# A matmul's opening: A's k-tiles 8 to 15 in two lots, B by two k-tiles, the bias loaded and added later

## The chip, the cores and the metric

One core of one Trainium2 chip. The metric is the device time of one execution in microseconds (us). The span in a profile counts from the first to the last instruction and is shorter: by 1.7 us in the runs of the kernel before. The times before spread little on the first chip (1781.77 to 1782.03 us).

## The reference

```python
a = randn(4096, 4096)      # float32
b = randn(4096, 4096)
bias = randn(4096)
out = tanh(a @ b + bias)
```

## The kernel before

fp16 matmuls of 128 x 128 by 128 x 512. B is worked in four chunks of 1024 columns, A in 32 row blocks of 128 rows, K in 32 k-tiles of 128. Row blocks are called 0 to 31. For the first chunk neither B nor A is there at the start, so the first eight row blocks are an **opening**: group 0 (row blocks 0 to 3) and group 1 (4 to 7) take the k-tiles in stretches as they land, and partial sums are set aside in SBUF (`spill`). All loads but those of B's first two k-tiles stand in one software queue issued by GpSimd (`want`, `want_a`), with at most eight in flight (counted from issue to landing in the trace of before, up to 95 us); VectorE transposes A (`turn`), adds partial sums (`add_aside`), adds the bias (`add_bias`) and the result (`end`). VectorE's timelines below show its instructions in the order of the program.

```python
    want_a("g0b", G, 0, G * Q, BL, BL)             # group 0, k-tiles 4-7
    want_a("g0c", G, 0, G * Q, KS, KM - KS)        # group 0, k-tiles 8-15, one lot
    for u in range(KS, KM, 2):
        want(lambda u=u: load_b_all(u, 2))         # B by two k-tiles, four loads each
    want_a("g1c", 2, 4 * P, 2 * Q, KS, KM - KS)    # group 1, k-tiles 8-15
    want_a("g1d", 2, 6 * P, 2 * Q, KS, KM - KS)
    bias_bc = biasp.tile([P, NCW], fp32, name="bias_bc")
    want(lambda: load_bias(bias_bc, 0, nc.gpsimd))
    for t in (KM, KM + 8):                         # 16 and 24
        want_a(("g1", t), G, 4 * P, G * Q, t, 8)
        for u in range(t, t + 8, TB):
            want(lambda u=u: load_b_all(u, TB))    # B by four k-tiles
    for m in g0:
        want_a(("g0", m), 1, m * P, Q, KM, KT - KM)
    # ... cut ...
    one_by_one(ps, g1, KS, KM, KS)
    for t in (KM, KM + 8):
        for i in range(G):
            turn(ats[G + i], ("g1", t), i * Q, t, 8)
        for m in g1 if t == KM else g0:
            for j in range(J):
                add_bias(m, j)
        across(ps, g1, t, min(t + 8, KT - TB), KS)
    turn(ats[0], ("g0", 0), 0, KM, KT - KM)        # row block 0, k-tiles 16-31
    down(ps, g1, KT - TB, KT, end)                 # group 1's results
    # ... cut ...
    for m in g0:
        for j in range(J):
            ps = psum.tile([P, NB], fp32, name="ps")
            for t in range(KM, KT):
                mm(ps, ats[m], b_cur, t, j, t == KM, t == KT - 1)
            if m < G - 1 and j == 0:
                turn(ats[m + 1], ("g0", m + 1), 0, KM, KT - KM)
            elif m == G - 1:
                new_at(j)
            end(ps, m, j)
```

## Time and profile before

| | before |
|---|---|
| time, median of 3 | 1781.81 us |
| TensorE busy, of a span of 1780.2 us | 1774.4 us |
| steady start-to-start of two matmuls in the opening | 0.216 us |
| waits of TensorE in the opening after 25 us, beyond that step | 0.08 + 0.21 + 0.24 us |
| landing of row block 0's last k-tiles | 84.88 us |
| first matmul of row block 1 on k-tiles 16 to 31 | 98.22 us |

To read it: TensorE is the bound, and the whole question is how long it stands still in the first 119 us. Its timeline of the kernel before, 84 to 110 us (start, length, engine, line and operation), merges what follows without a break:

```profile
83.76 7.72 PE L138 MATMUL ps<-b,at 128*128 128x512 f16 x35
91.31 18.94 PE L138 MATMUL ps<-b,atx 128*128 128x512 f16 x87
```

The second line is row blocks 0 to 2 of group 0 on k-tiles 16 to 31, without a pause. A line with a pause before it would carry a bracket with its length and who ended it.

### The profile page before, as it was taken

How to read it: one execution, taken by the hardware profiler on the slowest of the kernel's cores; microseconds unless marked ns; L12 is line 12 of the kernel's file. 1: busy time of each engine (PE TensorE's matmuls, PEld its weight loads, DVE VectorE, ACT ScalarE, POOL GpSimd, SP SyncE). 2: the span in 40 equal slices, each digit the busy share in tenths (PEclk: the TensorE clock that was granted, in tenths of full speed). 3: DMA queues.
4: the chain of work that ended last, by engine and by line, in shares of the span. 5: the costliest groups of instructions: out<-in, count | busy, mean ns of one | idle time of the engine just before them, and what ended most of it. 6: DMA issues, size and time to landing. Idle time of an engine off the chain costs nothing.

```text
span 1780.2 us, 20854 instructions
## 1 busy us (share of the span) xinstructions
PE 1774.4 (100%) x8254; PEld 806.9 (45%) x8254; DVE 763.8 (43%) x680; ACT 173.2 (10%) x279; POOL 872.1 (49%) x1618
## 2 busy tenths in 40 slices
PE   9999999999999999999999999999999999999999
PEld 4444444444444444444444444444444444444444
DVE  3764353444344443444344443444344443444342
ACT  2011000000000000000000000000000000000001
POOL 7465566544466554444456554444544454444510
PEclk9999999999999999999999999999999999999999
DMA  9999999976999877767699987766776667766641
GB/s 186 203 189 178 168 166 169 140 124 109 165 165 173 148 115 115 119 114 121 113 177 165 170 137 115 119 115 109 129 117 120 107 114 115 120 114 109 116 77 42
DMA packets 281393, 238.94 MB, mean 134 GB/s; under 512 B 159056, under 2 KB 231760, under 8 KB 281296
## 3 DMA queue, kind: packets, MB, share of 16 engines
q0 software_dynamic: 243280, 167.88, 70.1%
q1 hardware_dynamic: 37728, 69.62, 11.0%
q8 instruction: 64, 1.05, 0.2%
q14 instruction: 33, 0.27, 0.0%
q10 hardware_dynamic: 288, 0.13, 0.0%
HBM read 337.64 MB, written 67.11 MB: 227 GB/s over the span
## 4 chain that ended last, share of the span: by engine, by line
PE 99%; DMA 0%; issue 0%; ACT 0%; POOL 0%; DVE 0%; DVEq 0%; POOLq 0%
PE ps L412 93%; PE ps L138 6%; DMA nat<-in_a_dram 0%; ACT o_sb L152 0%; PE tp L257 0%; POOL nat L246 0%; DVE o_sb L149 0%; DVEq L149 0%; POOLq L435 0%
## 5 line engine op out<-in xcount | busy, mean ns | idle before, releaser
L412 PE MATMUL ps<-b,at 128*128 128x512 f16 x7712 | 1657.8, 378 | 0.0
L90 POOL DMA_DIRECT2D an<-in_a_dram x1492 | 805.5, 547 | 796.6 <-DVE at L100 583.4
L412 PEld LDWEIGHTS <-at 128*128 128x128 f16 x7712 | 754.6, 98 | 903.3
L100 DVE STREAM_TRANSPOSE at<-an 128x512 f16<-128x512 f16 (+1 forms) x380 | 565.6, 1539 | 85.8 <-DMA an<-in_a_dram 85.8
L149 DVE TENSOR_TENSOR o_sb<-ps,bias_bc 128x512 f32<-128x512 f32 (+1 forms) x243 | 165.4, 683 | 897.7 <-PE ps L412 695.7
L152 ACT ACTIVATE o_sb<-o_sb 128x512 f32<-128x512 f32 (+1 forms) x243 | 151.8, 626 | 1499.1 <-DVE o_sb L149 1499.1
L73 POOL DMA_DIRECT2D b<-in_b_dram x104 | 56.2, 544 | 15.5 <-DMA an<-in_a_dram 8.4
L138 PE MATMUL ps<-b,atx 128*128 128x512 f16 x256 | 56.2, 379 | 0.0
L138 PE MATMUL ps<-b,at 128*128 128x512 f16 x256 | 55.7, 379 | 0.1
L138 PEld LDWEIGHTS <-at 128*128 128x128 f16 x256 | 25.0, 98 | 30.5 <-DVE spill L181 0.5
L138 PEld LDWEIGHTS <-atx 128*128 128x128 f16 x256 | 24.6, 98 | 30.1 <-DVE atx L100 0.9
L100 DVE STREAM_TRANSPOSE atx<-an 128x512 f16<-128x512 f16 (+2 forms) x12 | 16.3, 1399 | 13.0 <-DMA an<-in_a_dram 13.0
L69 POOL DMA_DIRECT2D b<-in_b_dram x12 | 7.8, 654 | 22.4 <-PE ps L412 22.3
L152 ACT ACTIVATE spill<-spill 128x512 f32<-128x512 f32 x16 | 9.9, 632 | 85.6 <-DVE spill L149 85.5
L149 DVE TENSOR_TENSOR spill<-ps,spill 128x512 f32<-128x512 f32 x16 | 10.4, 678 | 9.9 <-PE ps L138 9.9
L181 DVE TENSOR_TENSOR spill<-spill,bias_bc 128x512 f32<-128x512 f32 x16 | 9.7, 680 | 0.0
L173 ACT COPY spill<-ps 128x512 f32<-128x512 f32 x16 | 8.0, 623 | 12.9 <-PE ps L138 12.9
L228 PE MATMUL ps<-zeros 128*128 128x512 f16 (+1 forms) x14 | 4.7, 498 | 1.3 <-DVE zeros L221 1.3
L176 DVE TENSOR_TENSOR spill<-ps,spill 128x512 f32<-128x512 f32 x8 | 4.8, 670 | 0.0
L228 PEld LDWEIGHTS <-zeros 128*128 128x128 f16 x14 | 1.6, 130 | 3.7 <-issue 2.4
L239 DVE CAST b<-spill 128x1024 f16<-128x1024 f32 x1 | 0.8, 849 | 4.5 <-DMA spill<-in_b_dram 4.5
L246 POOL DMA_DIRECT2D nat<-in_a_dram x4 | 2.3, 587 | 0.8 <-POOLq L435 0.8
(14 smaller groups left out, 8.9 us busy)
## 6 DMA issues: line engine op xcount, KB each, us to landing
an<-in_a_dram POOLq DMA_DIRECT2D x480, 192.0 KB, 5.1
out_dram<-o_sb SPq DMA_DIRECT2D x239, 256.0 KB, 2.7
an<-in_a_dram POOLq DMA_DIRECT2D x960, 32.0 KB, 2.7
b<-in_b_dram POOLq DMA_DIRECT2D x94, 256.0 KB, 8.2
b<-in_b_dram POOLq DMA_DIRECT2D x6, 1024.0 KB, 13.5
an<-in_a_dram POOLq DMA_DIRECT2D x32, 128.0 KB, 5.6
out_dram<-spill SPq DMA_DIRECT2D x16, 256.0 KB, 5.9
an<-in_a_dram POOLq DMA_DIRECT2D x12, 256.0 KB, 8.2
```

Of the source, the lines that this page charges most:

```text
L69: queue.dma_start(out=dst, in_=src[:, ds(t0 % BL, nt), :])
L73: nc.gpsimd.dma_start(out=bt[t0 // TB][ds(q * QP, QP), ds(t0 % TB, nt), :], in_=src.rearrange("(t p) n -> p t n", p=QP),)
L90: nc.gpsimd.dma_start(out=an[ds(q * QP, QP), :, ds((t - t0) * QP, n * QP)], in_=src.rearrange("(mb p) k -> p mb k", p=QP),)
L100: nc.vector.transpose(at[:, ds(t, n), :].rearrange("P t (mb p) -> P mb t p", p=QP), an[:, ds(mb0, Q), ds((t - t0) * QP, n * QP)].rearrange ...
L138: nc.tensor.matmul(ps, at[:, t, :], bt[t // TB][:, t % TB, ts(j, NB)], start=start, stop=stop)
L149: nc.vector.tensor_tensor(out=o_sb[:, piece], in0=ps[:, piece], in1=addend[:, piece], op=mybir.AluOpType.add)
L152: nc.scalar.activation(o_sb[:, piece], o_sb[:, piece], mybir.ActivationFunctionType.Tanh)
L173: nc.scalar.copy(aside(m, j), ps)
L176: nc.vector.tensor_tensor(out=aside(m, j), in0=ps, in1=aside(m, j), op=mybir.AluOpType.add)
L181: nc.vector.tensor_tensor(out=aside(m, j), in0=aside(m, j), in1=bias_bc[:, ts(j, NB)], op=mybir.AluOpType.add)
L228: nc.tensor.matmul(ps[:, ds(0, w)], zeros[:, :P], zeros[:, :w], start=i == 0, stop=i == n - 1)
L412: nc.tensor.matmul(ps, at[:, t, :], b_cur[t // TB][:, t % TB, ds(c0, w)], start=t == 0, stop=t == KT - 1,)
```

## The change

The intent is to have each k-tile there before TensorE asks: group 0's k-tiles 8 to 15 in two lots with their share of B in between, B's k-tiles 16 to 19 and 24 to 27 in lots of two, and the bias out of the way of both, behind B's k-tile 27. Since the bias then lands late, its additions move too. The diff:

```diff
-    want_a("g0c", G, 0, G * Q, KS, KM - KS)
-    for u in range(KS, KM, 2):
-        want(lambda u=u: load_b_all(u, 2))
+    for t in (KS, KS + 4):
+        want_a(("g0", t), G, 0, G * Q, t, 4)
+        for u in (t, t + 2):
+            want(lambda u=u: load_b_all(u, 2))
...
-    want(lambda: load_bias(bias_bc, 0, nc.gpsimd))
     for t in (KM, KM + 8):
         want_a(("g1", t), G, 4 * P, G * Q, t, 8)
-        for u in range(t, t + 8, TB):
-            want(lambda u=u: load_b_all(u, TB))
+        for u in (t, t + 2):
+            want(lambda u=u: load_b_all(u, 2))
+        if t > KM:
+            want(lambda: load_bias(bias_bc, 0, nc.gpsimd))
+        want(lambda t=t: load_b_all(t + TB, TB))
...
-    for m in g0:
-        turn(ats[m], "g0c", m * Q, KS, KM - KS)
+    for t in (KS, KS + 4):
+        for m in g0:
+            turn(ats[m], ("g0", t), m * Q, t, 4)
...
-        for m in g1 if t == KM else g0:
-            for j in range(J):
-                add_bias(m, j)
         across(ps, g1, t, min(t + 8, KT - TB), KS)
+    for m in g1:
+        for j in range(J):
+            add_bias(m, j)
     turn(ats[0], ("g0", 0), 0, KM, KT - KM)
     down(ps, g1, KT - TB, KT, end)
+    for m in g0:
+        for j in range(J):
+            add_bias(m, j)
```

## The prediction

85.5 + 2.24 + 4.81 + 4.86 + 2.30 = 99.7, and with it the 1783.2 us, rests on the trace of before and on estimates from it. In that trace one bias addition lasts 0.685 us and the next starts after 0.60. The 0.72 us of part (1) is the mean step between landings of four loads of A with runs of 128 elements, 25.61 to 27.85 us. The DMA share is 1.24 in the mean from 25 to 90 us (1.10 to 1.30 by stretches). That what stands behind a load put later comes forward by its length, in part (3), was the estimate: about 2 us for the bias.

> **What bounds the kernel now.** I read the head of the page with the engine totals first:
>
> ```profile
> span 1780.2 us, 20854 instructions
> PE 1774.4 (100%) x8254; PEld 806.9 (45%) x8254; DVE 763.8 (43%) x680; ACT 173.2 (10%) x279; POOL 872.1 (49%) x1618
> ```
>
> Then the chain that ended last, in order of time (start, length, what ran):
>
> ```profile
> 9.79 25.99 PE ps L138 x120
> 35.78 0.05 issue
> 35.82 41.60 PE ps L138 x192
> 77.42 0.08 issue
> 77.50 41.60 PE ps L138 x192
> 119.10 1654.20 PE ps L412 x7680
> ```
>
> TensorE is busy for all but 5.8 us. From 9.79 us to the end the chain is matmuls, broken twice by less than 0.1 us. The breaks are a little wider in the start times of single matmuls, which otherwise stand 0.216 apart: 35.40 to 35.82 (0.43) and 77.05 to 77.50 (0.46). So the waits that an opening order can take away are 0.21 + 0.24 = 0.45 us. The kernel is bound by TensorE; an order of loads can win 0.45 us or lose what it newly exposes.
>
> What stands behind the two breaks is read from the landing records of the software queue's loads beside the program's waits. B's k-tiles 8 and 9 finish landing at 35.73 and the matmul starts at 35.82. B's k-tiles 24 to 27, one lot of four, land at 77.26 and the matmul starts at 77.50. The loads of the opening land back to back from about 25 to 90 us, so in that stretch the DMA engines are full and the order decides who waits. A (fp32 in HBM, 0.5 MB a load) takes 1.33 us a load, B in lots of two k-tiles 0.64, in lots of four 1.25.
>
> Next the VectorE timeline where the eight-row opening ends, 84 to 101 us (start, length, what, and idle time before it with who ended it), then GpSimd's in the same stretch:
>
> ```profile
> 85.07 2.31 DVE L100 STREAM_TRANSPOSE atx<-an 128x2048 f16<-128x2048 f16 x1 [3.85 <-DMA an<-in_a_dram]
> 87.31 4.90 DVE L149 TENSOR_TENSOR spill<-ps,spill 128x512 f32<-128x512 f32 x8
> 92.12 2.30 DVE L100 STREAM_TRANSPOSE atx<-an 128x2048 f16<-128x2048 f16 x1
> 94.97 0.69 DVE L149 TENSOR_TENSOR spill<-ps,spill 128x512 f32<-128x512 f32 x1 [0.55 <-PE ps L138]
> ```
>
> ```profile
> 94.72 4.30 POOL L90 DMA_DIRECT2D an<-in_a_dram  x8 [4.89 <-DVE atx L100]
> ```
>
> The reader is to see that VectorE has no pause from 85.07 to 94.42, and that it starts there only when a load lands. The second transpose makes row block 1's k-tiles 16 to 31. TensorE runs row block 0 from 91.31 for 32 matmuls and begins row block 1 at 91.31 + 32 x 0.216 = 98.2 us. Slack of that transpose: 98.2 - 94.4 = 3.8 us.
>
> [...] The trace agrees with 685 ns for one bias addition; but eight in a row take 4.86 us, one per 0.61 us, since each overlaps the next, so I use the trace's 4.86. [...] four landed in 25.61 to 27.85, 0.72 us each from the load before, against 1.33 / 2 = 0.67 for the same bytes in runs twice as long. [...]
>
> **The change part by part.**
>
> (1) Group 0's k-tiles 8 to 15 in two lots of four. Four A loads of 1.33 us become four of 0.72, then B 8 to 11 (8 x 0.64), then four A of 0.72, then B 12 to 15. Counting from the unchanged landing at 27.85: first A lot 27.85 + 2.9 = 30.7 (was 33.2), B 8 and 9 at 33.3 (was 35.73), B 10 and 11 at 35.8, second A lot 38.7, B 12 and 13 at 41.3, B 14 and 15 at 43.8. TensorE wants k-tile 8 at 35.6, so the first break of 0.21 us goes. It wants k-tile 12 at 35.6 + 32 x 0.216 = 42.5: margin 1.3 us. Four more transposes, of half the size, lie in VectorE's idle time (it stood 8.2 us idle before 46.16).
>
> (2) B by two k-tiles for 16 to 19 and 24 to 27: eight more loads; 16 x 0.64 against 8 x 1.25 is 0.2 us more of queue. In return k-tiles 24 and 25 no longer wait for 26 and 27.
>
> (3) The bias load goes from before B's k-tile 16 to behind k-tile 27. Four A loads before the bias, the bias and one after span 46.08 to 52.31; less 4 x 0.67 and 1.33 that leaves about 2.2 us for the bias. What lay between comes 2 us earlier: k-tiles 24 and 25 at about 72.5 to 73 instead of 77.26. The second break of 0.24 us goes. The bias itself lands at about 77 to 78.
>
> (4) Group 1's bias additions stand now behind the transposes of its k-tiles 24 to 31: they run from about 77.3 to 82.2, still before the transpose that waits for its load at 85. Hidden.
>
> (5) Group 0's bias additions stand now after the eight result additions of group 1 and **before the transpose for row block 1**, as the built order of VectorE shows. Before, they ran from 76.36 to 81.2, in idle time. Here they are put into the stretch without a pause.
>
> The sum for (5): the start is the landing of row block 0's last k-tiles, 84.9 before. The queue holds the same bytes up to it, plus the slower A runs (8 x 0.72 - 4 x 1.33 = 0.4) and the smaller B lots (0.2): I take VectorE's start at 85.5 (85.07 + 0.4, halfway to the full 0.6). Transpose to result additions 2.24 (87.31 - 85.07), result additions to the next instruction 4.81 (92.12 - 87.31), bias additions 4.86, transpose 2.30: 85.5 + 14.2 = 99.7; matmul about 0.1 later, 99.8. Before it was 98.2. So row block 1 starts **1.6 us later than before**. The 0.45 us won earlier does not come off this: TensorE only arrives sooner at the same wait, which lasts about 99.8 - 97.8 = 2.0 us.
>
> After that the shift stays. The transpose also frees the buffer for the loads of the next row (the 94.72 line), so these go out 5 us later. They landed at 109.4 and were taken at 112.84; landing at 114.4, they are transposed by about 119.1, and TensorE wants the last piece at about 122. The row after that was transposed at 120.99 to 125.5 and wanted at 132.8; 5 us later still fits. From there the old slack comes back and the main loop has the same instructions.
>
> Total: 1781.81 + 1.6 = 1783.4; I take 0.2 off, for the chance that the load lands as early as it did: **1783.2 us**.
>
> **The rivals.**
>
> A. A small gain. If VectorE's additions of group 0 fitted before 98 us, the two breaks would be won: 1781.4. For it: the change plainly aims at both breaks. Against it: 14.2 us of VectorE work from a start that a full DMA queue sets at 85; the load would have to land by 83.5.
>
> B. A new wait for A's second lot at k-tile 12, or for the first result addition of group 0 at 49.5 (VectorE must first transpose the load that lands at about 46.5: done 48.9, first addition 49.5, about the time TensorE asks). Up to 1.5 us of such waits vanish in the wait at row block 1, so they would show in the trace and not in the time. Over that they add: 1784 to 1785.
>
> C. The bias itself becomes the bound: it would have to land after about 80, so that group 1's additions ran past 85 and pushed the whole VectorE chain. Its place in the queue says 77 to 78. It would add its lateness one for one.
>
> D. The late loads of the first ordinary rows leave TensorE waiting at 119 or 133 us. Margins by the sums above are some 3 us; if both were eaten, 1785 or more.
>
> **Range and chances.** The spread of the three runs before is 0.25 us, so the range is my error in the landing at 85 (give or take 0.7) and the rivals: B, C and D upward, A downward. 1781.8 to 1784.6 should hold it 8 times in 10. Two per cent is 36 us; nothing here is of that size: within 2% 0.98, 0.01 on each side.
>
> **What would show it right or wrong.** Right: no break of TensorE near 35.8 and 77.5; one gap of about 2 us near 98 us, ended by the transpose for row block 1; on VectorE eight bias additions between the result additions and that transpose; bias landing near 77; rows of the main loop unchanged. Wrong in step 1 if there is a gap near 42 us; in step 3 or 4 if the transpose at 85 waits for bias additions rather than for its load; in step 5 if the gap near 98 us is missing or is ended by a load; in the last step if gaps show at 119 or later, or if the time differs from 1781.8 by other than the gaps' sum.

## The result, and the profile after

The changed kernel takes **1785.95 us** in the median of four runs (1783.95 to 1786.53) against 1781.91 us of the kernel before: 4.0 us more. Ratio 1.0021, 95% interval 1.0003 to 1.0038: within 2%, as foretold, but the median lies 1.35 us above the top of the range. A ratio here is the mean time of one kernel's fast runs over that of the other's of the same rounds, so it is not quite the ratio of the medians quoted. A second thing is new: the runs spread over 2.6 us, those of before over 0.3.

The head of the page after, which answers to the two lines the prediction showed:

```profile
span 1783.6 us, 20876 instructions
PE 1774.5 (99%) x8254; PEld 806.0 (45%) x8254; DVE 763.5 (43%) x684; ACT 172.6 (10%) x279; POOL 875.6 (49%) x1630
```

TensorE has the same work, 1774.5 us; the span grew by 3.4 us. So all of that growth is standing still. The chain that ended last, its end:

```profile
99.25 2.31 DVE atx L100
101.57 0.04 issue
101.61 20.89 PE ps L138 x96
122.51 1654.20 PE ps L419 x7680
```

From 101.61 us on it is matmuls without a break, and the main loop takes 1654.20 us, to the digit what it took before. Before, the chain was matmuls from 9.79 us on; now it hands over to TensorE only at 101.61, from a transpose. VectorE's timeline after (start, length, what, idle time before it and who ended it), beside which the prediction's four lines of before are to be held:

```profile
80.57 4.91 DVE L181 TENSOR_TENSOR spill<-spill,bias_bc 128x512 f32<-128x512 f32 x8 [4.34 <-DMA bias_bc<-in_bias_dram]
87.45 2.31 DVE L100 STREAM_TRANSPOSE atx<-an 128x2048 f16<-128x2048 f16 x1 [1.98 <-DMA an<-in_a_dram]
89.69 4.84 DVE L149 TENSOR_TENSOR spill<-ps,spill 128x512 f32<-128x512 f32 x8
94.45 4.89 DVE L181 TENSOR_TENSOR spill<-spill,bias_bc 128x512 f32<-128x512 f32 x8
99.25 2.30 DVE L100 STREAM_TRANSPOSE atx<-an 128x2048 f16<-128x2048 f16 x1
```

Line 4 is the new link: group 0's eight bias additions stand between the result additions and the transpose for row block 1. And the chain starts at 87.45, not at 85.07. TensorE's timeline after:

```profile
29.01 20.89 PE L138 MATMUL ps<-b,atx 128*128 128x512 f16 x96 [0.24 <-DVE atx L100]
50.50 33.83 PE L138 MATMUL ps<-b,at 128*128 128x512 f16 x156 [0.59 <-DVE spill L176]
...
101.61 8.59 PE L138 MATMUL ps<-b,atx 128*128 128x512 f16 x39 [2.61 <-DVE atx L100]
```

The breaks at 35.8 and 77.5 us are gone. There are three pauses now: at 29.0 (0.40 us beyond the step from start to start), at 50.5 (0.75) and at 101.61 (2.77). Only the last counts in the end: 101.61 - 98.22 = 3.39 us is the whole growth of the span. The profiled run took 1785.70 us, 3.8 more than before: these 3.4 and the 0.4 outside the span. All four runs list a granted clock (the share of TensorE's full clock that was granted, in the mean of the run) of 1.0, which matters further down.

### The profile page after: what moved, and what is told of

Its sections match the earlier page's. It is cut to its first block, busy times and chain, and to the rows that moved or that the text cites. A ratio compares the mean times of both kernels' runs of the same rounds, so it can differ in the third digit from the quotient of the medians.

```text
span 1783.6 us, 20876 instructions
## 1 busy us (share of the span) xinstructions
PE 1774.5 (99%) x8254; PEld 806.0 (45%) x8254; DVE 763.5 (43%) x684; ACT 172.6 (10%) x279; POOL 875.6 (49%) x1630
## 3 DMA queue, kind: packets, MB, share of 16 engines
q8 instruction: 64, 1.05, 0.2%
## 4 chain that ended last, share of the span: by engine, by line
PE 94%; DMA 3%; POOL 1%; DVE 1%; issue 1%; ACT 0%; DVEq 0%; POOLq 0%
PE ps L419 93%; DMA an<-in_a_dram 2%; PE ps L138 1%; DMA b<-in_b_dram 1%; POOL an L90 1%; DMA bias_bc<-in_bias_dram 0%; DVE atx L100 0%; DVE spill L181 0%; POOL b L73 0%; POOL nat L246 0%; DVE spill L149 0%; POOL b L69 0%; ACT o_sb L152 0%; DVE o_sb L149 0%; POOL ident L263 0%
## 5 line engine op out<-in xcount | busy, mean ns | idle before, releaser
L73 POOL DMA_DIRECT2D b<-in_b_dram x112 | 60.2, 541 | 11.8 <-DMA an<-in_a_dram 6.9
L100 DVE STREAM_TRANSPOSE atx<-an 128x512 f16<-128x512 f16 (+1 forms) x16 | 16.7, 1085 | 14.2 <-DMA an<-in_a_dram 14.2
L69 POOL DMA_DIRECT2D b<-in_b_dram x12 | 7.8, 653 | 15.9 <-PE ps L419 15.7
```

The lines of the kernel that those rows point to most:

```text
L69: queue.dma_start(out=dst, in_=src[:, ds(t0 % BL, nt), :])
L73: nc.gpsimd.dma_start(out=bt[t0 // TB][ds(q * QP, QP), ds(t0 % TB, nt), :], in_=src.rearrange("(t p) n -> p t n", p=QP),)
L100: nc.vector.transpose(at[:, ds(t, n), :].rearrange("P t (mb p) -> P mb t p", p=QP), an[:, ds(mb0, Q), ds((t - t0) * QP, n * QP)].rearrange ...
```

## The experiments

Fifteen runs were made, some of them of the same kernel. "m1" is the first matmul of row block 1 on k-tiles 16 to 31; "landing" is the last landing of row block 0's k-tiles 16 to 31, from the landing records. All gave correct results. Each run also lists its mean granted clock. The profiles with one spell of 3.41 us at half clock have 0.999, `longer` with 6.83 us has 0.998, all others round to 1.0: so the list tells of such a spell in unprofiled runs too.

### The changed kernel again: `again` and `again2`

No edit.

> The changed kernel once more, unaltered, for its spread. Theory (a landing that jitters now sits on the path): the times differ from run to run by 1 us or more while those of the kernel before stay within 0.4 us; the profile has one TensorE gap near 98 us, and its length follows the landing of row block 0's k-tiles 16 to 31 (landing + about 14.3 us = first matmul of row block 1). Rival (the main loop is disturbed): the gap keeps its length of 2.8 us and the rest of the difference lies after 119 us.

> The changed kernel a third time, beside the next run on the same chip. Theory: 2.5 to 4 us over the kernel before; in the profile row block 1 starts 14.3 us after row block 0's last k-tiles land. Rival: another length than 14.3 us, or a difference after 119 us.

Measured: 1785.64 us (1784.61 to 1788.72) against 1782.34, and 1786.75 us (1784.50 to 1787.89) against 1782.19; ratios 1.0021 and 1.0022. Two expectations missed: the kernel before spread over 2.25 us beside `again`, not 0.4, and `again2` was 4.6 us slower, not 2.5 to 4. In the three profiles of the changed kernel the landing was at 87.33, 86.25 and 87.41 us and m1 at 101.61, 100.53 and 101.69 us: m1 follows the landing by 14.28, 14.28 and 14.28 us. So a landing that jitters by 1 us sits on the path. But the third profile showed more, TensorE's granted clock (columns of the views: stretch, its length, busy time and count of each engine, then the clock as PEclk, DMA share, GB/s). First the profile of `again2`, then the first profile of the changed kernel:

```profile
100.00:102.00 2.00, 0.31 (x2) 0.14 (x3) 2.00 (x2) 0.00 (x0) 0.07 (x1) 0.96 0.20 77
102.00:104.00 2.00, 2.00 (x6) 0.74 (x5) 2.00 (x3) 1.23 (x2) 2.00 (x4) 0.50 0.30 33
104.00:106.00 2.00, 2.00 (x8) 0.77 (x7) 1.02 (x1) 0.00 (x0) 2.00 (x5) 0.69 0.79 188
```

```profile
102.00:104.00 2.00, 2.00 (x11) 0.88 (x9) 2.00 (x3) 1.23 (x2) 2.00 (x5) 1.00 0.33 39
```

In `again2` the clock falls to 0.50 at 101.84 us for 3.41 us: six matmuls in 2 us where eleven should be. From m1 to the last matmul it takes 1.68 us more than in the first profile (1679.98 against 1678.30). This was in no theory of mine; the last experiments are about it. By the listed clocks 4 of the 14 runs of the changed kernel had one such spell (0.999): 1786.31, 1787.46, 1787.89 and 1788.72 us. The ten without it lie between 1783.95 and 1786.75.

### Additions deferred, loads as changed: `defer`

```diff
     down(ps, g1, KT - TB, KT, end)
-    for m in g0:
-        for j in range(J):
-            add_bias(m, j)
...
                 new_at(j)
+            add_bias(m, j)
             end(ps, m, j)
```

> Loads exactly as in the changed kernel, but each of group 0's eight bias additions stands just before its own result addition instead of before the transpose of row block 1. Theory (VectorE's order with the late landing makes the gap): the gap near 98 us is gone, the small ones near 28 and 50 us stay (some 0.4 and 0.8 us), 1781.5 to 1782.8 us, spread under 0.7 us. Rival (the reordered loads alone hold TensorE back): 1784.5 us or more, as in the changed kernel.

Measured: 1783.27 us (1783.22 to 1783.71) against 1782.34; ratio 1.0004, interval 0.9991 to 1.0017. Its landing was 87.25 us, as late as in the changed kernel, but TensorE does not wait at row block 1:

```profile
50.93 41.60 PE L138 MATMUL ps<-b,at 128*128 128x512 f16 x192 [1.18 <-DVE spill L176]
92.36 27.79 PE L138 MATMUL ps<-b,atx 128*128 128x512 f16 x128
```

The 128 matmuls of row blocks 0 to 3 run through. The loss and the spread go with VectorE's order; the late loads alone don't hold TensorE there. The median is 0.5 us above my range: the pause near 50 us was 1.34 us, not 0.8, and this order no longer hides it. Of the 0.9 us over the kernel before, 0.4 lie outside the span.

### Additions moved, loads as before: `adds_only`

```diff
-        for m in g1 if t == KM else g0:
-            for j in range(J):
-                add_bias(m, j)
         across(ps, g1, t, min(t + 8, KT - TB), KS)
+    for m in g1:
+        for j in range(J):
+            add_bias(m, j)
     turn(ats[0], ("g0", 0), 0, KM, KT - KM)
     down(ps, g1, KT - TB, KT, end)
+    for m in g0:
+        for j in range(J):
+            add_bias(m, j)
```

> Loads exactly as in the kernel before, only the bias additions stand where the change puts them. Theory: VectorE starts at about 85.1 us as before, 14.2 us of work in a row, row block 1 at about 99.4 us instead of 98.2: 1782.6 to 1783.8 us, so about a third of the loss; the rest is the later landing. Rival (the additions cost nothing without the late loads): 1781.9 us.

Measured: 1783.39 us (1782.79 to 1783.84) against 1782.34, 1.05 us more; the interval 0.9991 to 1.0016 holds 1. In the profile:

```profile
78.34 13.97 PE L138 MATMUL ps<-b,at 128*128 128x512 f16 x64 [0.79 <-DMA b<-in_b_dram]
92.15 7.07 PE L138 MATMUL ps<-b,atx 128*128 128x512 f16 x32
100.13 4.06 PE L138 MATMUL ps<-b,atx 128*128 128x512 f16 x18 [0.91 <-DVE atx L100]
```

Landing 85.71, m1 100.13: 14.42 us apart. So the moved additions alone make the pause at row block 1, here a short one. Two further points: this kernel has the loads of the kernel before, yet its landing is 0.83 us later than in the one profile of before that I had built on; and the second break, 0.24 us there, is 0.95 us here.

### The two lots alone: `split_only`

```diff
-    want_a("g0c", G, 0, G * Q, KS, KM - KS)
-    for u in range(KS, KM, 2):
-        want(lambda u=u: load_b_all(u, 2))
+    for t in (KS, KS + 4):
+        want_a(("g0", t), G, 0, G * Q, t, 4)
+        for u in (t, t + 2):
+            want(lambda u=u: load_b_all(u, 2))
```

(and the transposes in two lots to match)

> The kernel before with group 0's k-tiles 8 to 15 in two lots, B's loads between them, nothing else. Theory (the shorter runs of A cost the full queue 1 us): the break at 35.8 us goes, but the queue behind runs about 1 us later, so a gap of 0.5 to 0.8 us shows near 50 us and the break near 77.5 us grows to about 0.5 to 1 us: 1782.3 to 1783.3 us. Rival (splitting is free and only wins the break): 1781.6 to 1781.8 us.

Measured: 1783.29 us (1782.62 to 1783.60) against 1782.34, interval 0.9990 to 1.0015. The break at 35.8 is gone and a pause of 1.10 us stands at 50.8, ended by the first addition of a partial sum of group 0, which stands behind the transpose of a load that lands later with two lots (47.37 us in the changed kernel, which has this pause too, against 46.08 in the kernel before); the break at 78.8 is 0.33 us. The lots win one break and pay with another; 0.4 of the 0.95 us over the kernel before lie outside the span, as in every kernel with two lots but `longer`.

### One lot, the rest as changed: `no_split`, `no_split2`, `no_split_defer2`

The `split_only` edit undone in the changed kernel. The label of the third misleads: it is this same kernel once more, one look, state unknown, nothing deferred.

> The changed kernel with group 0's k-tiles 8 to 15 loaded and transposed in one lot again; everything else as changed. Theory (the two lots cost the full queue about 1 us): row block 0's last k-tiles land at 86.0 to 86.6 us, row block 1 starts 14.3 us after that landing, no gap near 50 us, the break of 0.2 us at 35.9 is back; about 1 us less than the changed kernel, 1784.0 to 1785.0 us. Rival (the B lots and the late bias make the landing late): landing still at 87 us or later and the time that of the changed kernel, 1785.6 us.

> The variant with k-tiles 8 to 15 in one lot again, since its first measurement (4.6 us over before) stands against the expectation and its profile began 1.1 us late with cold matmuls. Theory (a late start was the cause, and one lot saves the queue 0.7 us): 2 to 3.5 us over the kernel before and not above the changed kernel of the same call. Rival (one lot itself makes the landing later): again 4 us or more over before, and over the changed kernel.

> A second look at the one-lot variant of the run above, for its landing times alone. Theory: from the landing of the last of B's k-tiles 4 to 7 to the last of k-tiles 8 to 15, 15.8 to 16.1 us, against 16.0 to 16.9 us in two lots; row block 1 starts 14.3 us after row block 0's landing. Rival: no difference between one lot and two.

Measured: 1787.02 us (1785.78 to 1788.06) against 1782.45; 1786.01 us (1784.27 to 1786.89) against 1782.19, the changed kernel having 1786.75 us in that call; and 1783.99 us. The first is a miss: 1 us less than the changed kernel was expected, and 1.1 to 1.4 us more than its medians until then came. Its profile (the fastest of its five runs) began with the first load of A landing at 7.58 us instead of 6.2 to 6.7, a pause before that, and the clock at 0.5 from 8.64 to 12.05 us; row block 0's landing came at 87.70 us, not at 86.0 to 86.6. All five runs list a clock of 0.999, so each had one spell at half clock; where the unprofiled four had it is not recorded. The second is 3.8 us over the kernel before, a little more than the 3.5 expected, with the spell in three of its five runs, and not above the changed kernel, though the spreads overlap. The landing was 86.80 and 85.88 us in the later two profiles, and m1 14.35 us behind it in both.

What the lots cost the queue can be read better from all traces: from the last landing of group 0's k-tiles 4 to 7 to the last of B's k-tile 15 it took 16.60 us in the mean of nine profiles with two lots (16.02 to 17.67) and 15.91 in eight with one (15.52 to 16.42). So two lots cost **0.7 us**, where my prediction had 0.4. Whether it is the shorter runs or the doubled number of loads, no run separates.

### One lot and deferred additions: `no_split_defer`, `one_lot_defer`

The edits of `no_split` and `defer` together: of the change there remain B by two, the late bias and group 1's later additions. The same kernel twice.

> The same with group 0's bias additions put before their own result additions: B by two k-tiles, bias late, A in one lot. Theory: no gap at 50, at 77.5 or at 98 us, only the break of 0.2 us at 35.9 is left, so it is as fast as or a little faster than the kernel before: 0.2 to 0.8 us less in the median, and a narrower spread, since the 2 us of slack at k-tile 24 absorb late landings. Rival (some other cost of the late bias or of the smaller lots): 0.5 us or more slower than before.

> The variant with A in one lot, B by two, bias late and each addition just before its result addition, measured again: its first measurement was 0.9 us under the kernel before, inside the noise. Theory (it has slack at k-tile 24 and at row block 1 and needs no clock luck): 0.3 to 1 us under the kernel before again, all runs below 1782.8 us. Rival (no gain): medians equal within 0.2 us.

Measured: 1781.56 us (1781.50 to 1782.33) against 1782.45, ratio 0.9998; and 1781.65 us (1781.31 to 1782.49) against 1782.62, ratio 0.9997, interval 0.9983 to 1.0010. TensorE in the second:

```profile
28.50 21.13 PE L138 MATMUL ps<-b,atx 128*128 128x512 f16 x96
49.47 41.60 PE L138 MATMUL ps<-b,at 128*128 128x512 f16 x192
90.91 27.79 PE L138 MATMUL ps<-b,atx 128*128 128x512 f16 x128
```

Of the pauses only one of 0.24 us at 35.7, hidden in the first line, is left. Both medians are 0.9 to 1.0 us under the kernel before and all ten runs lie within 1.2 us; but both intervals hold 1, so a gain over the kernel before is likely and not shown. It is the best version that I found.

### Half of the additions: `half`

```diff
-    for m in g0:
+    for m in g0[:2]:
         for j in range(J):
             add_bias(m, j)
...
                 new_at(j)
+            if m >= 2:
+                add_bias(m, j)
             end(ps, m, j)
```

> The changed kernel with only half of group 0's bias additions (row blocks 0 and 1) before the transpose, the others before their own result additions. Theory (a chain on VectorE, 0.61 us per addition): row block 1 starts 14.3 - 4 x 0.61 = 11.9 us after the landing of row block 0's last k-tiles, so the gap near 98 us falls from 2 to 2.8 us to 0 to 0.6 us; median 1783.3 to 1784.3 us. Rival (a landing, not the additions, ends that wait): the gap stays at 2 us or more.

Measured: 1783.01 us (1781.72 to 1783.65) against 1782.45. VectorE's timeline:

```profile
85.36 2.31 DVE L100 STREAM_TRANSPOSE atx<-an 128x2048 f16<-128x2048 f16 x1 [1.92 <-DMA an<-in_a_dram]
87.60 4.84 DVE L149 TENSOR_TENSOR spill<-ps,spill 128x512 f32<-128x512 f32 x8
92.36 2.48 DVE L181 TENSOR_TENSOR spill<-spill,bias_bc 128x512 f32<-128x512 f32 x4
94.76 2.30 DVE L100 STREAM_TRANSPOSE atx<-an 128x2048 f16<-128x2048 f16 x1
```

Four additions take 2.48 us, and the transpose ends at 97.06 us, 11.8 us after the landing at 85.24; TensorE, which comes to row block 1 at 97.62, does not wait. The dose acts as the chain says, with the reserve that this profile had the earliest landing of all the experiments (its first load of A landed early, at 6.19 us); the median lies 0.3 us under the range I gave.

### The bias early again: `bias_early`

```diff
+    want(lambda: load_bias(bias_bc, 0, nc.gpsimd))
     for t in (KM, KM + 8):
...
-        if t > KM:
-            want(lambda: load_bias(bias_bc, 0, nc.gpsimd))
```

> The changed kernel with the bias load back in its old place in the queue, before B's k-tile 16; the additions stay late. Theory (the queue in front of row block 0's load holds the same bytes either way): landing 86 to 87.5 us, row block 1 starts 14.3 us later, time as the changed kernel, 1784.8 to 1786 us; only the start of group 1's additions moves, from about 80 to about 76 us. Rival (the bias in the late place costs the queue more): landing 0.5 to 1 us earlier and 1784 to 1785 us.

Measured: 1784.18 us (1783.43 to 1786.04) against 1782.45, interval 1.0000 to 1.0025; landing 86.62, m1 100.91 (14.29 behind). The median is 0.6 us under the theory's range and in the rival's, the landing fits both, and the spread covers both (its highest run lists the low clock): inconclusive by time. By the landing records of all traces the late place saves 1.66 us ahead of B's k-tile 16 (11.53 us in the mean of twelve profiles from B's k-tile 15 to group 1's k-tiles 16 to 23, against 13.19 of five) and costs 1.86 us behind (12.27 against 10.41 us): 0.2 us net, with single executions from 11.50 to 13.24.

### B by two alone: `two_only`

```diff
-        for u in range(t, t + 8, TB):
-            want(lambda u=u: load_b_all(u, TB))
+        for u in (t, t + 2):
+            want(lambda u=u: load_b_all(u, 2))
+        want(lambda t=t: load_b_all(t + TB, TB))
```

> The kernel before with B's k-tiles 16 to 19 and 24 to 27 by two and nothing else. Theory (this part alone is pure gain, as the additions stay early and A in one lot): the break at 77.5 us goes, the one at 35.8 us stays: 0.1 to 0.9 us less than before, the more the later the landings of its runs. Rival (more and smaller loads cost the queue): 0.3 us or more slower.

Measured: 1782.23 us (1781.79 to 1783.53) against 1782.19, ratio 1.0000: neither. In its profile the break at 77.5 is gone, those at 36.5 (0.22) and near 50.7 (0.46) remain. The landing was 86.92 us, 2.04 later than in the profile of before, at no cost: its additions are early. What it wins is no more than what a run's landings differ by.

### The pause bridged and lengthened: `bridge`, `longer`

`bridge` lets TensorE multiply a tile of zeros in the pause; `longer` adds four additions to VectorE's chain, into a tile that nobody reads.

```diff
                 mm(ps, ats[m], b_cur, t, j, t == KM, t == KT - 1)
+            if (m, j) == (0, J - 1):
+                fill(8, NB)
```

```diff
     for m in g0:
         for j in range(J):
             add_bias(m, j)
+    scratch = singles.tile([P, NB], fp32, name="scratch")
+    for _ in range(4):
+        nc.vector.tensor_tensor(out=scratch, in0=bias_bc[:, ts(0, NB)],
+                                in1=bias_bc[:, ts(1, NB)], op=mybir.AluOpType.add)
```

> The changed kernel with eight matmuls on a tile of zeros (8 x 0.216 = 1.7 us of work nobody needs) between row block 0 and row block 1, where TensorE waits for 2 to 3 us. Theory (part of the loss and most of the spread is a granted clock of 0.5 for 3.4 us that a long enough pause brings on in some executions, worth 1.7 us): no clock below 1.0 near 102 us, row block 1 still 14.3 us after the landing, median 1784.3 to 1785.4 us and none above 1786.3 us. Rival (the spread is all from the landings): median 1785.6 to 1786.7 us and single runs of 1787 us and more, as in the changed kernel.

> The changed kernel with four more additions of the same size, into a scratch tile, before the transpose of row block 1. Theory (VectorE chain plus clock): row block 1 starts 14.3 + 4 x 0.61 = 16.7 us after the landing, so the pause is about 5 us, long enough to lower the clock in every execution: 2.4 us for the additions and 1.7 us for the clock, 1787.8 to 1789.8 us, and a clock of 0.5 for 3.4 us in the profile. Rival (no link between pause and clock): 1787 to 1788.5 us with the clock at 1.0.

Measured: `bridge` 1785.11 us (1783.71 to 1785.51), `longer` 1790.46 us (1789.79 to 1791.19), both against 1782.62. TensorE in `bridge`:

```profile
92.45 7.07 PE L138 MATMUL ps<-b,atx 128*128 128x512 f16 x32
99.36 1.89 PE L228 MATMUL ps<-zeros 128*128 128x512 f16 x8
101.43 8.81 PE L138 MATMUL ps<-b,atx 128*128 128x512 f16 x40 [0.18 <-DVE atx L100]
```

m1 is still 14.28 us behind the landing (87.15), the clock stays at 1.0, and no run is above 1785.51, where the changed kernel had single runs of 1786 to 1788.7. `longer` by stretches, columns as above:

```profile
100.00:102.00 2.00, 0.00 (x0) 0.00 (x0) 1.97 (x3) 0.00 (x0) 0.00 (x0) 0.94 0.01 2
102.00:104.00 2.00, 0.33 (x1) 0.13 (x2) 2.00 (x2) 0.00 (x0) 0.09 (x1) 0.50 0.00 0
104.00:106.00 2.00, 2.00 (x6) 0.73 (x5) 2.00 (x3) 1.23 (x2) 2.00 (x4) 0.50 0.31 34
106.00:108.00 2.00, 2.00 (x6) 0.67 (x5) 1.01 (x1) 0.00 (x0) 2.00 (x5) 0.50 0.68 153
```

The pause is 5.27 us and the clock is at 0.5 for 6.83 us, two spells of 3.41. m1 came 17.05 us after the landing, 2.77 more than the 14.28 of the changed kernel: the added additions cost 0.69 us each, not 0.61. They all write one tile; that each waits for the one before on that account is my reading, which no run tests. It is slower than expected since I had reckoned with one spell. All five runs of `longer` list 0.998, all five of `bridge` 1.0, where the changed kernel had the spell in 4 of 14: lengthening the pause brings the low clock on in every run, and that shows the link. `bridge` alone would not, since ten of 14 runs have no spell anyway.

Why some pauses do it and others don't: in the traces the clock rises and falls at instants that lie whole multiples of 3.413 us apart (in `again2` from the rise at 6.27 to the fall at 101.84 there are 28 of them; in the kernel before 520 from 4.92 to 1779.85, in the changed kernel 521 from 4.88 to 1783.22). If that grid is taken for the edges of windows, which is my reading, the idle time within one window, worked out from the start times, was 2.49 us in `again2` and 3.01 in `no_split2`, which both lost the clock; 1.91 in `again`, 1.83 in `no_split_defer2`, and at most 1.61 in the first profile (its 2.77 us are cut by an edge at 100.45), which kept it. A threshold does not follow: the opening of `no_split` lost the clock after a window with a pause of 2.04 us and some shorter ones, and `longer` stayed low for a second window with 1.93. The low spells after these pauses lasted 3.41 us (twice that in `longer`) at a clock of 0.5, and a pause shorter than that, 2.49 us in `again2`, was enough.

## Why the prediction was wrong

**What bounds the kernel, and the breaks to be won** (0.45 us): right. Both breaks are gone in the profile after.

**Steps 1 to 4.** Right in kind. K-tile 12 caused no pause; the transposes and group 1's additions stayed hidden. Rival B's pause near 50 us did come (0.75 us) and did vanish in the later one, as foretold (so did one of 0.40 us at 29.0, which I had not foreseen and which `adds_only`, with the loads of before, has too); `defer` and `split_only`, which have no later pause, show what it is worth. The bias landed at 80.48 rather than 77 to 78 us, but 85.5 us, where the additions of group 1 ended, was still before the landing at 87.3, so rival C stayed out.

**Step 5, the mechanism**: right, and precisely. The chain from the start of VectorE to m1 was 14.16 us (87.45 to 101.61), predicted 14.2 and 0.1. `adds_only`, `defer` and `half` show that it is this order which makes the pause.

**Step 5, the start of the chain, "I take VectorE's start at 85.5"**: this term was mis-sized. It was 87.45 us. Against the 84.88 us of before, the landing came 2.45 us later, where the queue's extra work was put at 0.6 and 0.4 of it used (called halfway, which would be 0.3). In that one trace 0.99 us come from the stretch with the two lots (0.7 in the mean of all traces), 1.08 net from the bias in its late place (0.2 in the mean), 0.1 from B's lots (0.4 in the mean, for k-tiles 16 to 23), and 0.3 from a start of the queue that was later. So the change itself costs the landing about 1.3 us by the means; the rest is that the one execution of before was early and this one late: the same loads landed between 85.24 and 87.41 us in seven profiles (`half` to `again2`), 86.75 in the mean. The deeper fault: I anchored the term on a single execution of a kernel in which that landing had 3.8 us of slack, so that its jitter did not show in the times, and I took the narrow spread of those times as the spread of the landing. `adds_only`, with the very same loads, landed 0.83 us later. Of the 3.4 us by which m1 moved in the profiled run, 1.6 were foretold and this term is the other 1.8. The rest of the way from 1783.2 to 1785.95 is, to 0.15 us, the 0.2 taken off for luck, the 0.4 outside the span, which no step of mine had, and a median 0.25 above the profiled run.

**The last step, "after that the shift stays"**: right for the loads of the next rows (rival D stayed out; the main loop took the same 1654.20 us), but it missed a cost: TensorE's granted clock falls for 3.41 us after some of these pauses, and in `again2` that cost 1.68 us. No rival of mine had it. It has no share in the 4.0 us: all four runs of the first measurement list a clock of 1.0. It is in the three highest runs of `again` and `again2` (1787.46 to 1788.72 us, listed with 0.999).

**The range** followed the same fault: give or take 0.7 us for the landing, where the same loads landed over 2.2 us, and nothing for the clock.

## What to carry to other kernels

On VectorE an instruction put ahead of another cost its whole length once VectorE had no pause left before the point where TensorE asked: eight additions put m1 14.28 us behind the landing, four had the transpose done 11.8 us behind it (`half`); so put additions just ahead of their use, as `defer` does (1783.27 us against 1785.95), not in front of a transpose that feeds the matmuls. Before moving work behind a landing, ask how much that landing varies between executions: slack hides the variation, and taking the slack away makes it part of the time (in `two_only` a landing at 86.92 us, 2.04 later than in the profile of before, cost nothing; in the changed kernel m1 came 14.28 us behind the landing whether that was at 86.25 or at 87.41 us). And a pause on TensorE may cost well over its length, since the clock can follow: 1.68 us on top of 2.49 in `again2`.

## What stays open

- What in a pause brings the low clock on. By the grid above, pauses of 2.49 us (`again2`) and 3.01 us (`no_split2`) that lay within one window halved the clock for 3.41 us, while a pause of 1.91 us within one window (`again`), and one of 2.77 us cut by a window's edge (the changed kernel), did not. What counts is therefore not the length of the gap alone.
- Runs of 512 B read and 256 B written cost 16.60 against 15.91 us for a stretch of the same bytes in which A came in half as many loads with runs twice as long; the number of loads is not separated from the length of the runs.
- In the kernel before, packets of 16 KB of the queue called instruction start at 46.59 and 74.77 us, and shortly after them the loads that land at 49.16 and 77.26 come 1.74 and 1.78 us after the landing before, where their like take 0.67 and 1.25. After such a packet at 21.36 us there is no such delay (1.24 to 1.37 us a landing). This was seen side by side, not tested, and the second delay is not in every profile.
